# Two of seven half-size products of a down projection, each split once more into seven quarter-size products

## The chip, the cores and the metric

The kernel runs on one core of a Trainium2 chip. The engines of a core that matter here are TensorE (PE: matrix products; its weight loads are listed apart as PEld), VectorE (DVE), ScalarE (ACT) and GpSimd (POOL), each with a queue of instructions that it works off in order. SyncE (SP) only issues DMA transfers; POOL issues some too. The metric is the time of one execution on the device, in microseconds (us).

## The reference

One step of an encoder layer for 1024 prompt frames and 32 sample frames, 1056 tokens of width 1024. The layer ends in the squared-ReLU MLP with 4096 hidden features:

```python
def trunk_layer(x, ...):
    h = rms_norm(x, g_mix)
    z = h @ w_in                      # attention, convolution and gates
    ...
    x = x + (jax.nn.sigmoid(ga) * a + jax.nn.sigmoid(gb) * bo) @ w_mix_out
    ...
    x = x + co @ w_co                 # cross-attention
    hm = rms_norm(x, g_mlp)
    x = x + jnp.square(jax.nn.relu(hm @ w_up)) @ w_down
```

A last RMS norm gives the output. Everything is float32. The change is in the last line's product with `w_down`, 4096 by 1024.

## The kernel before

**Precision.** A float32 matrix product is made of three passes of a faster format: every operand is split into a high part (ACT casts it) and a low part (DVE subtracts the cast from the original), and TensorE sums high times high, high times low and low times high. `split`, lines 128 to 130, does so for the weights, `split_here`, lines 1316 to 1320, for an operand of the down projection in place.

**Layout.** Features lie on the 128 partitions, tokens along the row. In the down projection the tokens are two halves of `HT` = 528 columns, each of two quarters of `QT` = 264. A weight tile is 128 x 1024 floats (512 KB), eight blocks of 128 x 128.

**Seven half-size products.** Inner dimension (4096), outputs (1024) and tokens are halved. The eight products of halves are replaced by seven of sums of halves (Winograd's form of Strassen's scheme). The activations of each product are one of seven operands, named in `KINDS`: `b11`, `b21`, `b22` are halves themselves, `n1`, `n3`, `n4`, `t2` are sums. The up projection writes them to device memory (`op_d`), 16 tiles of 128 x 528 for each. The weights are a raw quarter of `w_down` (for `b11`, `b21`, `n4`) or a sum from `wsum_d` (for the others). `stage` (from line 1874) queues one product: 4 output tiles `j` times 2 halves `t` of the inner dimension, one weight tile for each of these eight steps, 48 matmuls with one weight tile (`part`, lines 1801 to 1811: 2 token quarters, 8 inner tiles, 3 passes). After the second half of a `j`, `to_x1` (from line 1788) adds the PSUM banks into the residual `x1` or subtracts them there, once for each place that the product belongs to; DVE does it, in up to three pieces for each since the residual is tiled in 384 tokens. Where a piece completes the residual, its square is added up for the last norm (ACT squares, POOL adds, lines 274 and 276).

**What runs beside it.** During a product, `pump2` fetches the operands of the next one by SyncE, three tiles a step, and splits them: per product 16 casts on ACT and 16 subtractions on DVE. `dslots` gives them their SBUF slots, alternating between two sets.

**Weights.** `next_w` keeps up to three split weights ready (`wh` and `wl` have three buffers each). `fetch_w` loads a raw tile into `wr`, which has two buffers here, on SyncE's queue (line 159).

**Sums of weights.** POOL makes them early, beside attention and gates: `pieces` (lines 708 to 710) lists 14 pieces for the gates, 32 for the down projection and 4 for the up projection. Each call of `sum_step` (lines 718 to 741) issues the load of one new piece and then, for the piece loaded by the call before, four additions and the store. Two tiles alternate: `ws`, and `xacc`, which later holds the sums of squares. All these instructions are pinned to their order among themselves. The 32 `hosts` (lines 743 to 777), one for each unit of attention, call it once each from the fourth on, on the second of three token chunks; later the output projection of attention and the gates call it again. `after_gates` ends this phase; then conv output and mix (`do_conv_out`, `do_mix`) use POOL for an addition for each tile (line 1069).

The order of instructions on each engine is made by a scheduler ahead of the run, from the order of the program text and estimated times; on the chip it is fixed.

## Time and profile before

| | us |
|---|---|
| three runs | 1746.15, 1753.02, 1753.42 |
| their median | 1753.02 |
| span of the profiled execution, first to last instruction | 1747.8 |
| ScalarE busy in it | 852.9 |
| GpSimd busy in it | 586.2 |
| VectorE busy in it | 1188.1 |

The down projection is the end of the span: its first matmul (line 1809) starts at 1400.6 us and its last at 1735.9 us; what follows is the last norm and the output. Its 2688 matmuls are 7 times 384. In a row of the profile, "idle before" is the time that the engine stood still just ahead of these instructions, with what ended most of it; a tile's name is written without its number, so `n` stands for `n1`, `n3` and `n4`. In a row of a timeline, the first number is the start in us from the begin of the span and the second the duration.

### The profile page before, as it was taken

The numbers are of one execution on the slowest core, as the hardware profiler recorded it, in microseconds if no ns is written. First come the engines' busy times: TensorE is split into PE (matmuls) and PEld (weight loads), VectorE is DVE, ScalarE is ACT, GpSimd is POOL, SyncE is SP. The second block draws the span as 40 slices with busy tenths as digits, with TensorE's granted clock in tenths as the row PEclk, the third lists the DMA queues.
The fourth block names the chain that finished last, engine by engine and source line by source line (L and its number), as shares of the span: only waits on it lengthen the run. The fifth ranks groups of instructions, "written<-read, shape, count | busy, mean of one in ns | idle before, by whom it ended". The sixth has DMA issues, their size and how long they took to land. (4 is left out here: it accounts for less than half of the span.)

```text
span 1747.8 us, 32606 instructions
## 1 busy us (share of the span) xinstructions
PE 1727.7 (99%) x12262; PEld 1712.4 (98%) x12262; DVE 1188.1 (68%) x2276; ACT 852.9 (49%) x1660; POOL 586.2 (34%) x667
## 2 busy tenths in 40 slices
PE   9999999999999999999999999999999999999998
PEld 8999999999999999999999999999999999999998
DVE  7776777768666646555677888787666686545675
ACT  8653534535335324434556666765444463332444
POOL 0026366443553544432224232005555410000121
PEclk9999999999999999999999999999999999999999
DMA  4333344333436888867766667775666695555554
GB/s 185 104 126 128 114 134 153 115 139 127 160 132 204 296 292 280 291 203 238 264 213 198 221 227 241 235 258 191 217 222 219 219 330 185 188 193 169 192 170 160
DMA packets 179854, 346.60 MB, mean 198 GB/s; under 512 B 18657, under 2 KB 101249, under 8 KB 179569
## 3 DMA queue, kind: packets, MB, share of 16 engines
q1 hardware_dynamic: 163504, 290.07, 50.0%
q0 software_dynamic: 15568, 53.68, 8.8%
q8 instruction: 96, 1.57, 0.4%
q10 hardware_dynamic: 624, 0.77, 0.1%
q14 instruction: 62, 0.50, 0.1%
HBM read 250.73 MB, written 93.14 MB: 197 GB/s over the span
## 5 line engine op out<-in xcount | busy, mean ns | idle before, releaser
L129 ACT CAST wh<-wr 128x1024 fp32r<-128x1024 f32 (+1 forms) x214 | 223.8, 1046 | 366.6 <-PE acc L1810 121.4
L130 DVE TENSOR_TENSOR wl<-wr,wh 128x1024 fp32r<-128x1024 f32 (+1 forms) x214 | 275.0, 1285 | 106.2 <-ACT wh L129 105.4
L200 PE MATMUL acc<-X,wh 128*128 128x384 f32 (+1 forms) x864 | 281.5, 326 | 0.0
L201 PE MATMUL acc<-X,wh 128*128 128x384 f32 (+1 forms) x864 | 278.8, 323 | 0.1
L202 PE MATMUL acc<-X,wl 128*128 128x384 f32 (+1 forms) x864 | 277.8, 322 | 0.0
L276 POOL TENSOR_TENSOR xacc<-xacc,ct 128x384 f32<-128x384 f32 (+1 forms) x56 | 75.6, 1354 | 379.9 <-ACT ct L274 378.1
L201 PEld LDWEIGHTS acc<-X,wh 128*128 128x128 f32 x864 | 162.7, 188 | 1.7 <-DVE X L280 0.7
L200 PEld LDWEIGHTS acc<-X,wh 128*128 128x128 f32 x864 | 162.4, 188 | 0.8
L202 PEld LDWEIGHTS acc<-X,wl 128*128 128x128 f32 x864 | 162.4, 188 | 0.1
L200 PE MATMUL acc<-Y,wh 128*128 128x384 f32 (+1 forms) x432 | 139.9, 326 | 3.2 <-DVE ct L1068 2.9
L202 PE MATMUL acc<-Y,wl 128*128 128x384 f32 (+1 forms) x432 | 140.0, 325 | 2.7 <-DMA wl<-wl_d 2.7
L201 PE MATMUL acc<-Y,wh 128*128 128x384 f32 (+1 forms) x432 | 139.7, 324 | 0.0
L129 ACT CAST PTh<-pt 128x512 fp32r<-128x512 f32 (+3 forms) x94 | 45.8, 516 | 112.8 <-PE pt L598 111.4
L1809 PE MATMUL acc<-n,wh 128*128 128x264 f32 x352 | 100.2, 285 | 0.0
L1810 PE MATMUL acc<-n,wh 128*128 128x264 f32 x352 | 100.1, 284 | 0.0
L1811 PE MATMUL acc<-n,wl 128*128 128x264 f32 x352 | 99.9, 284 | 0.0
L735 POOL TENSOR_TENSOR ws<-ws 128x256 f32<-128x256 f32 x100 | 89.5, 895 | 5.6
L735 POOL TENSOR_TENSOR xacc<-xacc 128x256 f32<-128x256 f32 x100 | 86.8, 868 | 5.7 <-DMA xacc<-in_w_in 0.4
L200 PEld LDWEIGHTS acc<-Y,wh 128*128 128x128 f32 x432 | 81.4, 189 | 4.4 <-DVE ct L1068 3.8
L202 PEld LDWEIGHTS acc<-Y,wl 128*128 128x128 f32 x432 | 81.5, 189 | 3.0 <-DMA wl<-wl_d 3.0
L201 PEld LDWEIGHTS acc<-Y,wh 128*128 128x128 f32 x432 | 81.6, 189 | 0.0
L584 ACT ACTIVATE S<-S,nmx 128x257 f32<-128x257 f32 (+1 forms) x132 | 64.2, 488 | 18.9 <-DVE nmx L579 17.6
(432 smaller groups left out, 5554.9 us busy)
## 6 DMA issues: line engine op xcount, KB each, us to landing
wr<-in_w_up SPq DMA_DIRECT2D x53, 512.0 KB, 4.5
wr<-in_w_in SPq DMA_DIRECT2D x52, 512.0 KB, 3.6
wr<-wsum_d SPq DMA_DIRECT2D x40, 512.0 KB, 3.5
wr<-in_w_conv_out SPq DMA_DIRECT2D x24, 512.0 KB, 3.9
wr<-in_w_mix SPq DMA_DIRECT2D x24, 512.0 KB, 5.2
wr<-in_w_down SPq DMA_DIRECT2D x24, 512.0 KB, 3.6
n_d<-Z SPq DMA_DIRECT2D x32, 264.0 KB, 4.2
xacc<-in_w_down POOLq DMA_DIRECT2D x16, 512.0 KB, 4.5
```

The source lines that it names most:

```text
L129: act.copy(hi, src)
L130: dve.tensor_sub(lo, src, hi.bitcast(F32))
L200: pe.matmul(out, wh[:, a], hi, start=(k == 0), stop=False)
L201: pe.matmul(out, wh[:, a], lo, start=False, stop=False)
L202: pe.matmul(out, wl[:, a], hi, start=False, stop=(k == len(acts) - 1))
L276: pool_e.tensor_tensor(acc, acc, sq, op=ALU.add)
L584: act.activation(stl[:, h, : nk + 1], stl[:, h, : nk + 1], AF.Exp, scale=-1.0, bias=nmx[:, h : h + 1], accum_out=den[:, h : h + 1],)
L735: pin(pool_e.tensor_tensor(t[:, to], t[:, x], t[:, y], op=ALU.add))
L1809: pe.matmul(a, wh[:, s], hi, start=(t == 0 and k == 0), stop=False, skip_group_check=True)
L1810: pe.matmul(a, wh[:, s], lo, start=False, stop=False, skip_group_check=True)
L1811: pe.matmul(a, wl[:, s], hi, start=False, stop=(t == 1 and k == 7), skip_group_check=True)
```

## The change

Products `b21` and `n4` are computed by the same scheme once more: inner dimension, outputs and tokens of the product are halved again, and seven quarter-size products P1 to P7 (8 inner tiles, 2 output tiles `i`, 264 tokens) take the place of eight. These two are products with a raw quarter of `w_down` that go to one place of the residual only. `t2` now comes ahead of `n4`: a product of the old kind stands before each.

- **More sums of weights.** 16 pieces (`w2`), made by the same `sum_step` with subtractions, stored in `w2_d`. Every second host from the sixth on gets a second call, on the third chunk: 14 calls.
- **Sums of operands.** During the product before (`b11`, `t2`), all 16 operand tiles are fetched in the first four steps (`prepare`); POOL makes three differences of quarters for each pair (`first_sums`) and writes them back by its own DMAs in place of the raw quarters; the first eight tiles are split (`near_split`), the two other sums go to tiles of their own (`extra_split`). That product runs its outputs in pairs, as `b11` did already: the first half of its operands is used for the last time two steps before its end.
- **The recursed stage** (`stage2`): 14 items, one weight tile each, 24 matmuls each. Sums of products that share a bank are made by accumulating into it; DVE or ACT takes a partial sum out in between (`after`). Beside them (`beside`) come the last sums of operands on POOL, their split, the raw quarters' split, and from the seventh item on the fetches for the next product.
- **Low halves on POOL.** `far_split` casts on ACT and subtracts on POOL: four tiles in each recursed stage, and eight of the 16 of the product behind it (`t2`, `n3`).
- Slots are given by tables (`HOMES`, `EXTRA`) in place of `dslots`.

```diff
+    RAW2 = {"b21": 1, "n4": 3}
+    w2_d = {kind: dram.tile([2, 4, P, 4, 256], F32, name=f"w2_{kind}") for kind in RAW2}
...
+    pieces += [("w2", kind, i, b) for kind in RAW2 for i in range(2) for b in range(4)]
...
+            elif at[0] == "w2":
+                _, kind, i, b = at
+                for r in range(2):
+                    pin(pool_e.dma_start(t[:, 2 * r : 2 * r + 2], io["w_down"][i + 2 * r, :, b, :, RAW2[kind]].rearrange("t p c -> p t c")))
...
-            for to, x, y in ((3, 2, 3), (2, 0, 2), (0, 0, 3), (1, 1, 0)):
-                pin(pool_e.tensor_tensor(t[:, to], t[:, x], t[:, y], op=ALU.add))
+            for to, x, y in ((3, 2, 3), (2, 0, 2), (0, 3, 0), (1, 1, 0)):
+                op = ALU.subtract if at[0] == "w2" and to != 3 else ALU.add
+                pin(pool_e.tensor_tensor(t[:, to], t[:, x], t[:, y], op=op))
...
+        if i % 2 and i > 4:
+            extras.append((2, sum_step))
...
-    KINDS = ["b11", "b21", "n4", "t2", "n3", "n1", "b22"]
+    KINDS = ["b11", "b21", "t2", "n4", "n3", "n1", "b22"]
...
+    def far_split(hi, lo):
+        raw = lo.bitcast(F32)
+        pin(act.copy(hi, raw))
+        pin(pool_e.tensor_tensor(lo, raw, hi.bitcast(F32), op=ALU.subtract))
...
+    def first_sums(kind, k):
+        (h0, x0), (h1, x1_) = ((hi.bitcast(F32), lo.bitcast(F32)) for hi, lo in (dn[kind, k], dn[kind, 8 + k]))
+        t = W["pool"].tile([P, 4, 256], F32, tag="ws", name=nm("ws")).rearrange("p q c -> p (q c)")[:, : 3 * QT]
+        t3, t2, t4 = (t[:, i * QT : i * QT + QT] for i in range(3))
+        pin(pool_e.tensor_tensor(t3, quarter(x1_, 1), quarter(x0, 1), op=ALU.subtract))
+        pin(pool_e.dma_start(quarter(x0, 1), t3))
+        pin(pool_e.tensor_tensor(t2, t3, quarter(x0, 0), op=ALU.add))
+        pin(pool_e.tensor_tensor(t4, quarter(x1_, 0), t2, op=ALU.subtract))
+        pin(pool_e.dma_start(h1, t[:, QT:]))
+    def extra_split(kind, k):
+        hi, lo = dn[kind, "e", k] = dpair(homes(EXTRA[kind])[k])
+        src = dn[kind, 8 + k][0].bitcast(F32)
+        pin(act.copy(hi, src))
+        pin(dve.tensor_sub(lo, src, hi.bitcast(F32)))
+    def last_sums(kind, m):
+        hi, lo = dn[kind, "f", m] = dpair(homes(EXTRA[kind])[8 + m])
+        for q in range(2):
+            h1, x1_ = (x.bitcast(F32) for x in dn[kind, 8 + 2 * m + q])
+            t = tmp(QT)
+            pool_e.tensor_tensor(t, quarter(x1_, 1), quarter(h1, 0), op=ALU.subtract)
+            pool_e.dma_start(quarter(lo.bitcast(F32), q), t)
+        return lambda: split_here(hi, lo)
...
+    def prepare(kind):
+        pairs = [(k, 8 + k) for k in range(8)]
+        at = {n: [] for n in range(8)}
+        for n in range(4):
+            at[n].append(lambda n=n: [fetch_op(kind, x) for pair in pairs[2 * n : 2 * n + 2] for x in pair])
+            at[n].append(lambda n=n: [first_sums(kind, k) for k in (2 * n, 2 * n + 1)])
+            at[n + 3].append(lambda n=n: [near_split(kind, k) for k in (2 * n, 2 * n + 1)])
+        for n in range(2):
+            at[6 + n].append(lambda n=n: [extra_split(kind, k) for k in range(4 * n, 4 * n + 4)])
+        return at
...
+    def stage2(kind, h, f0, last):
...
+        into = {"P1": "A", "P2": "A", "P6": "B", "P7": "B", "P4": "B", "P5": "C", "P3": "C"}
...
+        def beside(n):
+            if n < 2:
+                splits.extend(last_sums(kind, m) for m in (2 * n, 2 * n + 1))
+            elif 7 <= n < 9:
+                splits.pop(0)()
+                splits.pop(0)()
+            if 2 <= n < 6:
+                for k in (2 * n - 4, 2 * n - 3):
+                    (split_here if n < 4 else far_split)(*dn[kind, 8 + k])
+            if n == 4:
+                wanted2.extend((nxt, k) for k in range(16))
+            if 6 <= n:
+                pump2(2)
+        n = 0
+        for p in ("P1", "P6", "P7", "P4", "P2", "P5", "P3"):
+            for i in range(2):
+                def fn(w, p=p, i=i, n=n):
...
+                    for k in range(8):
+                        hi, lo = operand2(kind, p, k)
+                        s = slice(k * P, k * P + P)
+                        pe.matmul(a, wh[:, s], hi, start=(p in ("P1", "P6", "P5") and k == 0), stop=False, skip_group_check=True)
+                        pe.matmul(a, wh[:, s], lo, start=False, stop=False, skip_group_check=True)
+                        pe.matmul(a, wl[:, s], hi, start=False, stop=(k == 7), skip_group_check=True)
+                    after(p, i)
+                    beside(n)
...
-    stage("b21", ("w_down", 1), ((*A11, True, True),))
-    stage("n4", ("w_down", 3), ((*A21, True, False),))
+    stage2("b21", *A11, True)
     stage("t2", ("w_sum", 0), ((*A12, False, False), (*A21, True, False), (*A22, True, False)))
+    stage2("n4", *A21, False)
```

102 lines of the change are left out of this document (81 added, 21 removed).

## The prediction

> **What bounds the kernel now.** I began with the page: span, busy shares.
>
> ```profile
> span 1747.8 us, 32606 instructions
> ...
> PE 1727.7 (99%) x12262; PEld 1712.4 (98%) x12262; DVE 1188.1 (68%) x2276; ACT 852.9 (49%) x1660; POOL 586.2 (34%) x667
> ```
>
> TensorE sets the time. A busy share says little of pace, since ends are modelled, so I cut the down projection into stretches of 46.6 us, about one half-size product each (the first still holds the tail of the up projection; columns: stretch, then busy time and count of PE, PEld, DVE, ACT, POOL, then clock, DMA share, GB/s).
>
> ```profile
> 1402.00:1448.60 46.60, 46.60 (x385) 46.60 (x384) 38.41 (x70) 27.10 (x43) 4.84 (x3) 1.00 0.94 330
> 1448.60:1495.20 46.60, 46.60 (x385) 46.60 (x384) 29.47 (x55) 19.06 (x28) 3.21 (x2) 1.00 0.51 166
> ```
>
> A product is 4 output tiles x 16 inner tiles x 2 token quarters x 3 passes = 384 matmuls, and 385 start in each stretch, up to an edge: 46.6 / 384 = 0.1214 us each, without a gap, at full clock. VectorE (DVE) has 8 and 17 us to spare, GpSimd (POOL) over 40. So removed matmuls shorten the time directly, as long as the other engines still feed TensorE.
>
> **What is removed.** Seven quarter-size products are 7 x 2 output tiles x 8 inner tiles x 3 passes = 336 matmuls for 384. Twice 48 are saved: 96 x 0.1214 = **11.7 us**. That is the whole possible gain, 0.67%.
>
> **What is added to the two stages.** A recursed stage lasts 336 x 0.1214 = 40.8 us of TensorE. The prices (busy us and mean ns; count and min/median/max in ns; start and us; last the first stretch again for L1793 alone, the adds into the residual on DVE):
>
> ```profile
> L130 DVE TENSOR_TENSOR wl<-wr,wh 128x1024 fp32r<-128x1024 f32 x63 | 77.8, 1235 | 49.6 <-ACT wh L129 49.3
> ...
> L1538 DVE TENSOR_TENSOR Z<-Z,pc 128x264 f32<-128x264 f32 x2 | 0.8, 426 | 0.0
> ...
> L1320 DVE TENSOR_TENSOR n<-n,n x44: 694/700/1830, 1404.3 to 1682.6; 128x528 fp32r<-128x528 f32 x44
> ...
> L735 POOL TENSOR_TENSOR ws<-ws x100: 725/746/1742, 155.4 to 766.4; 128x256 f32<-128x256 f32 x100
> L730 POOL DMA_DIRECT2D ws<-in_w_down x16: 533/533/685, 347.9 to 712.3; - x16
> ...
> 1210.92 1.33 POOL L1574 TENSOR_TENSOR lt<-lt,Z 128x528 f32<-128x528 f32 x1
> ...
> 1402.00:1448.60 46.60, 7.18 (x28) 1.00 0.94 330
> ```
>
> DVE, per recursed stage: 14 weight splits at 1.23 us (there were 8, since a weight tile now serves 24 matmuls, not 48) = 17.2; 16 operand splits of 528 columns at 0.70 (4 of the last sums, 4 raw, 8 for the next product) = 11.2; 10 adds of a bank and a kept partial sum at 0.43 = 4.3; 12 pieces into the residual at 7.18 / 28 = 0.26 = 3.1. Together 35.8 of 40.8 us, 88%. ScalarE (ACT) casts alongside and, at 27 of 46.6 us in its fullest stretch, has more room. POOL, nearly idle before: 8 subtractions of a quarter at 0.75 (the 256-column row stands in for 264) = 6.0, 12 low halves that `far_split` takes from DVE at 1.33 = 16.0, and 8 DMA issues at 0.53 to 0.69.
>
> Neither sum passes 40.8. Their sharing is the question. These rows of the timeline show pairs that overlapped (start, duration):
>
> ```profile
> 1221.39 2.20 POOL L1568 TENSOR_TENSOR Z<-lt,Z 128x528 f32<-128x528 f32 x1 [2.45 <-DVE Z L1564]
> ...
> 1222.32 1.84 DVE L1566 TENSOR_TENSOR Z<-lt,Z 128x528 f32<-128x528 f32 x1
> ...
> 1478.29 1.64 POOL L276 TENSOR_TENSOR xacc<-xacc,ct 128x384 f32<-128x384 f32 x1 [62.26 <-ACT ct L274]
> ...
> 1478.97 1.52 DVE L1320 TENSOR_TENSOR n<-n,n 128x528 fp32r<-128x528 f32 x1
> ...
> 1216.27 1.29 POOL L1469 TENSOR_TENSOR s<-wr,s 128x512 f32<-128x512 f32 x1
> ...
> 1216.31 0.71 DVE L1519 TENSOR_TENSOR Z<-acc,lt 128x528 f32<-128x528 f32 x1 [2.62 <-PE pc L882]
> ```
>
> A DVE operation with both sources in SBUF takes 0.70 alone, but 1.84 and 1.52 beside a POOL one: it ends 0.57 and 0.56 us after POOL does, so it ran when POOL was through. With a PSUM source (last pair) it stays at 0.71. I therefore **add** POOL's arithmetic to DVE's two-SBUF work: 17.2 + 11.2 + 2.6 (the 10 residual pieces that come from a temporary) = 31.0, and POOL's 22.0, make 53.0 us in 40.8. Eight of the far halves (10.6 us) belong to the next product's second half and can run over into its first 11.7 us: 42.4. In `b21`'s stage 4 accumulations of squares (L276; 1.64 less the 0.68 before DVE's start, 0.96 each) add 3.8: 46.2. Excess: 5.4 us for `b21`, 1.6 for `n4`.
>
> The lead that could swallow it:
>
> ```profile
> wr<-in_w_down SPq DMA_DIRECT2D x24, 512.0 KB, 3.6
> ...
> 1459.17 1.05 ACT L129 CAST wh<-wr 128x1024 fp32r<-128x1024 f32 x1 [4.79 <-PE acc L1810]
> ```
>
> Today the cast waits for TensorE to give back a split tile, so splits run two tiles ahead: 2 x 24 x 0.1214 = 5.8 us less the split itself (2.3) is a lead of 3.5. A raw tile's round, issue to landing and split, is 3.6 + 1.05 + 1.23 = 5.9 us, over two raw tiles 2.94 us per weight against 2.91 wanted: this takes 14 x 0.03 = 0.4 of the lead and leaves no room for a late split. What waits in the end is a TensorE matmul on its `wl`, and all of TensorE's queue behind it. So `b21` stalls for 5.4 - 3.1 = 2.3 us and `n4` stays under its lead: **+2.3 us**. Bounds: 0 (DVE's order puts weights first) and 2 x (53.0 - 40.8) + 3.8 = 28.2 (nothing slides, no lead).
>
> **Preparation beside the product before.** POOL gets 24 subtractions (18.0 us) and 16 issues (8.8 at 0.55) into `b11`'s 46.6 us, and again into `t2`'s. DVE's count stays there: 16 splits for 16. In the first stretch DVE's 38.4 less 7.2 (residual adds, from PSUM), POOL's 4.8 of before and the new 18.0 make 54.0 in 46.6: 7.4 too much. Data are also late there: 330 GB/s x 46.6 us is 15.4 MB, and the writes back from SBUF to SBUF add 8 x 405 KB = 3.3 MB; at the highest rate near it,
>
> ```profile
> 1410.00:1420.00 10.00, 10.00 (x84) 10.00 (x83) 9.89 (x12) 6.62 (x11) 3.52 (x2) 1.00 1.05 388
> ```
>
> that is 18.7 / 388 = 48 us. The first quarter product needs all eight near splits within 3 us of its start. Of 0 to 7.4 I take **+3.0**, since much of DVE's work there is the tail of the up projection; in `t2`'s stretch, if like the second row (166 GB/s, 29.5 us of DVE), nothing. No wait is added on TensorE apart from these operands and the banks: the second sum into a bank waits for DVE's reading of the first, with 24 matmuls (2.9 us) between.
>
> At this place a rule of the Trainium skill speaks against the change. "SBUF — State Buffer", section "SBUF: two separate sides", says that a DMA issued by GpSimd can starve, because its descriptors can't be written while VectorE holds the shared port, and gives 3.1 us instead of 0.62. By it, 16 issues would take 50 us, an estimate from that page, and the preparation would miss its product. The L730 row has a largest issue of 0.685 us among 16, and the row of 117 to 523 us below has DVE 71% busy, so this trace doesn't show it; I keep it as rival 4.
>
> **The earlier stages.** Sixteen pieces of summed weights join the 50 that POOL makes beside attention and gates, each two loads, four additions and a store. SyncE's queue is not touched there. The chain:
>
> ```profile
> 277.33 1.45 POOL L728 DMA_DIRECT2D xacc<-in_w_in  x2 [2.93 <-DMA gsum_d<-xacc]
> 287.00 1.45 POOL L728 DMA_DIRECT2D ws<-in_w_in  x2 [2.57 <-DMA gsum_d<-ws]
> ...
> 802.09 1.00 POOL L1069 TENSOR_TENSOR ct<-ct,ct 128x384 f32<-128x384 f32 x1 [32.96 <-DMA wr<-in_w_conv_out]
> ...
> 117.00:523.00 406.00, 406.00 (x2627) 399.96 (x2627) 287.40 (x721) 172.43 (x426) 203.57 (x303) 1.00 0.40 133
> ...
> 844.87 0.51 ACT L274 ACTIVATE xacc<-Ga 128x384 f32<-128x384 f32 x1
> ```
>
> Back to back a step takes 9.7 us, and each load waits for a store's landing, with POOL's queue (the attention's small copies, the convolution's products) behind it. From 117 to 523 us 29 of the steps ran (by the timeline's loads), 281 us. POOL's other work there is 203.6 less 29 x 5.2 (four additions at 0.75, and issues of 1.1 to 2.9) = 53. That leaves 406 - 281 - 53 = 72 us, 7 steps; the other 9 come after the old end, 769 us (802.1 less the idle 33.0), at 769 + 87 = 856 us. TensorE itself has no slack, but nothing waits for these sums until 1448. What does wait is the tile: `xacc` is written at 844.9, and L1069 stands in POOL's queue from 802, then late behind blocked loads. Bounds: 0 (they fit between) and 8 convolution outputs each 4 us later, 32; by the row at 844.9, 11 us before that end, where a single cast waits and TensorE has convolution outputs beside it, I take **+1.0**.
>
> **Sum:** -11.7 + 2.3 + 3.0 + 1.0 = **-5.4 us** on a span of 1747.8. The three runs shown are 1746.15, 1753.02 and 1753.42: the span lies between, and what is around it isn't shown, so I carry the difference to the median: 1753.0 - 5.4 = **1747.6 us**. Half a per cent, about what a measurement of this kernel can tell from no change, is 8.8 us.
>
> **Rivals.**
> 1. *The lead holds and the preparation is in time: the whole gain stays.* For it: both engines are under 100% taken singly, and from 117 to 523 us POOL is busy half of the time and DVE 71% beside a full TensorE. Against: POOL's work there is not needed at once. Time: 1753.0 - 11.7 + 1 = 1742.3. Chance 0.31.
> 2. *VectorE and GpSimd in turn become the bound in both recursed stages* (slower). It decides where the far halves don't slide: 28.2 + 4.0 - 11.7 = +20.5, 1773.5; it passes no change once the stall is over 7.7 us, and 0.5% from 16.5. Chance 0.11.
> 3. *The chain of sums ends past the gates and holds the residual stage* (slower). It decides from the end of the chain at about 845 us: 8 x 4 = 32 for the 1.0 gives 1747.6 + 31 = 1779; half of it 1763. Chance 0.08.
> 4. *POOL's DMA issues starve behind DVE.* Each of 16 issues waits one weight split (1.23): 19.7 us late before `b21`, little before `n4`, whose stretch has 20 us free: 1747.6 + 19.7 - 3.0 = 1764. Chance 0.04.
>
> Forecast: partial stall, 0.46, its own range 1745 to 1758. Faster by over 0.5% is rival 1 (0.31), within is the forecast (0.46), slower is 2 to 4 (0.23). The range takes in rival 1, with half of the 7 us by which the runs above spread, rival 4 and the smaller half of 2 and 3: 1738 to 1768.
>
> **What would show it.** Right: 336 matmuls in each recursed stage, its length 41 to 47 us, DVE near 90%, POOL at half, TensorE waiting on `wl` there. Wrong: a length of 40.8 (rival 1); over 50, or overlapped splits of 2 us throughout (2); the chain's last store after 845 us and fewer matmuls per 10 us from 800 to 880 (3); POOL issues of over 1 us before `b21` (4). A stall in the attention hosts, which I cost at nothing because TensorE shows none and DVE has 119 of 406 us free, would be an error of mine.

## The result and the profile after

The changed kernel takes 1843.5 us (median of 5 runs, 1840.7 to 1846.1) where the kernel before takes 1746.2 (5 runs): a ratio of 1.054, 95% interval 1.052 to 1.056. The forecast was 1747.6, at most 1768. Rows of the changed kernel bear its own line numbers: `first_sums` is L1660 to L1664 (L1661 and L1664 issue its two write-backs), splits on ACT and DVE are L1334/1335, extra splits L1672/1673, weight splits L131/132, the recursed matmuls L2038 to 2040, their additions L2000 and L2009, the chain of sums L738 to L752, and POOL's addition in the convolution's output, L1069 before, is L1084.

The profiled execution has a span of 1839.0 us against 1747.8, 91.2 more. Two marks divide it: the first and the last matmul into `pc`, the up projection. They stand at 1174.50 and 1407.57 us before, and at 1191.82 and 1424.86 after. So **17.3 us** are lost ahead of the up projection, none in it, and **73.9 us** behind it, where 96 matmuls fewer should have given 11.7 back: 85.6 us of stall.

The first loss, in the timeline of the changed kernel (start, length, engine, line, operation; in brackets the idle time before and what ended it):

```profile
814.71 3.13 POOL L746 TENSOR_TENSOR ws<-ws 128x256 f32<-128x256 f32 x4
818.15 0.59 POOL L752 DMA_DIRECT2D w_n<-ws  x1 [0.31 <-POOL ws L746]
818.76 1.00 POOL L1084 TENSOR_TENSOR ct<-ct,ct 128x384 f32<-128x384 f32 x1
819.80 0.51 ACT L131 CAST M<-ct 128x384 fp32r<-128x384 f32 x1 [18.65 <-POOL ct L1084]
821.72 0.69 PE L205 MATMUL acc<-Y,wh 128*128 128x384 f32 x1 [10.52 <-ACT wh L131]
```

The chain of sums makes its last store at 818.15 us (before: 767.69), and only then does GpSimd reach the addition behind it, which ran at 802.09 before. ScalarE's queue stands for 18.65 us on that addition, with weight casts behind it, and TensorE for 10.52 on one of those casts.

The second loss, in the waits of TensorE from 1425 to 1660 us (waiter, what it waited for, us in total, times, longest):

```profile
PE acc L2038 <- ACT Z L1334: 24.6, 4, 8.0
PE acc L2038 <- ACT n L1334: 21.1, 4, 7.7
PE acc L2038 <- DVE ct L2000: 5.5, 8, 0.9
PE acc L2038 <- DVE ct L2009: 4.5, 2, 2.6
```

The recursed stages' first quarter products wait 45.7 us for the near splits. What those wait for shows in the timeline of GpSimd and ScalarE within the first of these stretches:

```profile
1483.78 0.55 POOL L1664 DMA_DIRECT2D H<-ws  x1 [0.41 <-POOL ws L1663]
1484.24 0.63 ACT L1334 CAST Z<-Z 128x528 fp32r<-128x528 f32 x1 [4.73 <-DMA Z<-ws]
1490.04 0.74 POOL L1660 TENSOR_TENSOR ws<-H,Z 128x264 f32<-128x264 f32 x1 [5.70 <-DMA H<-ws]
1493.85 0.63 ACT L1334 CAST Z<-Z 128x528 fp32r<-128x528 f32 x1 [3.30 <-DMA Z<-ws]
1494.87 0.56 POOL L1664 DMA_DIRECT2D H<-ws  x1 [0.41 <-POOL ws L1663]
1497.36 0.73 POOL L1660 TENSOR_TENSOR ws<-H,Z 128x264 f32<-128x264 f32 x1 [1.93 <-DMA H<-ws]
1504.90 0.73 POOL L1660 TENSOR_TENSOR ws<-H,Z 128x264 f32<-128x264 f32 x1 [2.14 <-issue]
```

The first sums of a pair start only when the write-back of the pair before has landed, since `ws` is one tile: 7.3 and 7.5 us from one start to the next in the last three rows of L1660, 13.5 ahead of them (the start before is at 1476.53), where the arithmetic is 2.3 us. That is not the whole of it: the first pair stands 8.0 us ahead of issuing its write-back, for a reason that the profile doesn't name. The eight pairs run from 1431.47 to 1509.73 us, 78 us, beside a product of 46.6; ahead of `n4` they run from 1573.57 to 1636.09, 62.5 us. Beside their ends TensorE stands, as the last four of these stretches of the changed kernel show; the first row lies in the first loss (stretch and length, then busy us and count of PE, PEld, DVE, ACT and POOL, granted clock, DMA share, GB/s):

```profile
810.00:820.00 10.00, 1.20 (x7) 0.88 (x6) 0.00 (x0) 0.20 (x1) 8.51 (x12) 0.67 0.37 136
...
1480.00:1490.00 10.00, 1.40 (x3) 0.79 (x3) 3.48 (x9) 0.71 (x2) 3.89 (x6) 0.62 0.78 260
1490.00:1500.00 10.00, 1.40 (x3) 0.79 (x3) 2.20 (x3) 1.82 (x3) 7.56 (x11) 0.50 0.14 54
1500.00:1510.00 10.00, 1.96 (x5) 1.11 (x5) 2.27 (x3) 2.52 (x5) 6.98 (x11) 0.50 0.22 82
...
1620.00:1630.00 10.00, 2.09 (x5) 1.29 (x5) 1.46 (x2) 1.26 (x2) 5.29 (x8) 0.50 0.40 145
```

A full stretch of the down projection has 84 matmuls; in the last four rows there are 3 to 5. There no engine is busy throughout, and the DMA share is as low as 0.14: a chain of short steps, each waiting for the one before, not a lack of throughput.

### The profile page after: what moved, and what is told of

It is laid out like the page before. It is cut to its first block, busy times and chain, and to the rows that moved or that the text cites. A ratio compares the mean times of both kernels' runs of the same rounds, so it can differ in the third digit from the quotient of the medians.

```text
span 1839.0 us, 32903 instructions
## 1 busy us (share of the span) xinstructions
PE 1739.7 (95%) x12166; PEld 1711.4 (93%) x12166; DVE 1251.1 (68%) x2308; ACT 881.9 (48%) x1700; POOL 788.0 (43%) x915
## 5 line engine op out<-in xcount | busy, mean ns | idle before, releaser
L131 ACT CAST wh<-wr 128x1024 fp32r<-128x1024 f32 (+1 forms) x226 | 236.1, 1045 | 324.8 <-PE acc L206 77.3
L132 DVE TENSOR_TENSOR wl<-wr,wh 128x1024 fp32r<-128x1024 f32 (+1 forms) x226 | 297.4, 1317 | 109.4 <-ACT wh L131 108.2
L746 POOL TENSOR_TENSOR ws<-ws 128x256 f32<-128x256 f32 x132 | 114.9, 870 | 7.0
L746 POOL TENSOR_TENSOR xacc<-xacc 128x256 f32<-128x256 f32 x132 | 111.4, 844 | 7.5 <-DMA xacc<-in_w_in 0.2
L131 ACT CAST PTh<-pt 128x512 fp32r<-128x512 f32 (+3 forms) x94 | 45.8, 517 | 104.7 <-PE pt L603 103.4
L1871 PE MATMUL acc<-n,wh 128*128 128x264 f32 x256 | 73.4, 287 | 0.0
L1870 PE MATMUL acc<-n,wh 128*128 128x264 f32 x256 | 73.3, 286 | 0.0
L1872 PE MATMUL acc<-n,wl 128*128 128x264 f32 x256 | 73.3, 286 | 0.0
```

The lines of the kernel that those rows point to most:

```text
L131: act.copy(hi, src)
L132: dve.tensor_sub(lo, src, hi.bitcast(F32))
L746: pin(pool_e.tensor_tensor(t[:, to], t[:, x], t[:, y], op=op))
L1870: pe.matmul(a, wh[:, s], hi, start=(t == 0 and k == 0), stop=False, skip_group_check=True)
L1871: pe.matmul(a, wh[:, s], lo, start=False, stop=False, skip_group_check=True)
L1872: pe.matmul(a, wl[:, s], hi, start=False, stop=(t == 1 and k == 7), skip_group_check=True)
```

## The experiments

One table first. "Up from" is the first matmul into `pc`, "up" the time to the last one, "rest" from there to the end of the span, all of the profiled execution, in us; the medians and ratios to the kernel before are of all runs. Among kernels whose early stages are alike, "up from" ranges by some 10 us (1190 to 1200), so a difference of a few us in that column says nothing. "Rest" differs by some 3 us where the down projection is alike (414.1 and 417.4, 361.3 and 364.5).

| kernel | up from | up | rest | median | ratio (95%) |
|---|---|---|---|---|---|
| before | 1174.5 | 233.1 | 340.2 | 1746.2 | |
| the change | 1191.8 | 233.0 | 414.1 | 1843.5 | 1.054 (1.052–1.056) |
| e1 sums only | 1207.6 | 233.1 | 340.2 | 1771.3 | 1.015 (1.012–1.019) |
| e2 two temporaries | 1196.4 | 233.0 | 387.2 | 1817.5 | 1.041 (1.039–1.043) |
| e3 in place | 1190.0 | 233.0 | 361.6 | 1789.3 | 1.025 (1.023–1.026) |
| e4 sums in the up projection | 1169.7 | 265.7 | 424.0 | 1864.1 | 1.067 (1.065–1.069) |
| e5 more calls | 1181.3 | 233.0 | 417.4 | 1833.3 | 1.049 (1.047–1.051) |
| e6 SyncE issues | 1190.5 | 233.1 | 406.5 | 1831.2 | 1.048 (1.046–1.050) |
| e7 in place, spread | 1196.9 | 233.0 | 361.3 | 1795.3 | 1.027 (1.025–1.029) |
| e8 e7 + calls | 1179.5 | 233.1 | 364.5 | 1782.4 | 1.020 (1.019–1.022) |
| e9 in place, no subtractions | 1190.9 | 233.0 | 358.8 | 1785.0 | 1.023 (1.020–1.026) |
| e10 in place, no first sums | 1193.7 | 233.0 | 362.1 | 1790.2 | 1.025 (1.023–1.028) |
| e11 both left out | 1192.5 | 233.0 | 358.7 | 1788.6 | 1.025 (1.022–1.029) |
| e12 in place, third raw tile | 1200.3 | 233.0 | 362.8 | 1791.1 | 1.025 (1.021–1.029) |
| e13 e8 + third raw tile | 1185.8 | 233.1 | 361.1 | 1777.7 | 1.017 (1.014–1.019) |
| e14 in place, one-bank tiles | 1197.8 | 233.0 | 366.8 | 1791.7 | 1.026 (1.023–1.029) |
| e15 e14 + third tile + calls | 1177.5 | 233.1 | 355.1 | 1775.5 | 1.017 (1.015–1.020) |
| e16 e2 + one-bank tiles + calls | 1182.0 | 233.1 | 386.4 | 1803.6 | 1.032 (1.029–1.034) |
| e17 e15, no subtractions | 1185.5 | 233.0 | 349.8 | 1769.0 | 1.012 (1.011–1.014) |

### The chain of sums: e1, e4, e5

e1 adds to the kernel before only the pieces and their calls, and uses none of them:

```
+    pieces += [("w2", kind, i, b) for kind in RAW2 for i in range(2) for b in range(4)]
...
+        if i % 2 and i > 4:
+            extras.append((2, sum_step))
```

> The kernel before, to which only the sixteen extra pieces of weight sums of the change are added, made and written to DRAM at the same places, and read by nothing; the down projection is that of before. Theory: the chain of sums on GpSimd, longer by sixteen pieces, ends past the first gates and holds back GpSimd's additions of the convolution, so this alone costs what the changed kernel is behind at the start of its up projection: 1746 + 15 to 18, that is 1761 to 1764, with the last store of the chain near 818 us. Rival: what is late there is caught up later, or the changed attention hosts have nothing to do with it: 1746 to 1750.

It took 1771.3 us, 24.6 over the 1746.6 of the kernel before beside it, with the same 340.2 us behind the up projection. The theory's mechanism holds and its price was too low; the rival falls. In the timeline of e1 (its L743, L749 and L1081 are the chain's addition and store and the convolution's addition):

```profile
826.27 3.13 POOL L743 TENSOR_TENSOR ws<-ws 128x256 f32<-128x256 f32 x4
829.72 0.59 POOL L749 DMA_DIRECT2D w_n<-ws  x1 [0.31 <-POOL ws L743]
830.33 1.00 POOL L1081 TENSOR_TENSOR ct<-ct,ct 128x384 f32<-128x384 f32 x1
```

The chain ends still later here than in the changed kernel, 829.7 instead of 818.2 us; why these two differ wasn't tried. The profiled execution is also the longest of e1's four, 1782.7 us where the others took 1767.4 to 1771.8, so its 33.1 us ahead of the up projection are more than the sums usually cost.

e4 takes the pieces out of the early stages and makes one at each pair of the up projection:

```
-    pieces += [("w2", kind, i, b) for kind in RAW2 for i in range(2) for b in range(4)]
+    pieces2 = [("w2", kind, i, b) for kind in RAW2 for i in range(2) for b in range(4)]
...
+        if i == 0:
+            pieces.extend(pieces2)
+        sum_step()
         c = [ps.tile([P, 512], F32, tag="pt", bufs=2, name=nm("pc"))[:, :QT] for _ in range(2)]
```

> The changed kernel, whose sixteen pieces of weight sums are made in the up projection, one at each of its pairs, in place of beside the attention and the first gates; the calls of the chain before are those of the kernel before. Theory: the late chain costs the changed kernel 15 to 18 us, and in the up projection the sums cost nothing: 1825 to 1828. Rival: GpSimd is needed as much in the up projection, and the loss only moves there: 1840 to 1846.

It took 1864.1 us, slower than both said. The early stages have their time back (the up projection starts at 1169.7, 22 us sooner than in the changed kernel), but the up projection grows by 32.6 us and what follows by 9.9. The stretch of the up projection in e4, then its longest entry in the waits of TensorE there, an entry in those of ScalarE, and VectorE's weight splits in e4 (1170 to 1436 us) and in the changed kernel (1192 to 1424 us; count, busy us, mean ns, idle before):

```profile
1175.00:1430.00 255.00, 231.80 (x1819) 227.34 (x1818) 173.70 (x190) 107.44 (x143) 206.89 (x183) 0.97 0.73 246
```

```profile
PE acc L895 <- DVE wl L1498: 17.1, 11, 4.1
```

```profile
ACT wh L1495 <- POOL s L1483: 13.4, 8, 2.3
```

```profile
L1498 DVE TENSOR_TENSOR wl<-s,wh 128x1024 fp32r<-128x1024 f32 x30 | 53.2, 1773 | 15.7 <-ACT wh L1495 15.7
```

```profile
L1500 DVE TENSOR_TENSOR wl<-s,wh 128x1024 fp32r<-128x1024 f32 x30 | 36.5, 1216 | 0.6 <-ACT wh L1497 0.6
```

GpSimd is busy for 207 of 255 us, and TensorE waits for VectorE's weight splits (L1498). They are late in two ways: each lasts 1.77 us instead of 1.22, and ScalarE's casts ahead of them wait 13.4 us for `s`, the sums of the up projection's own weights that GpSimd makes there, which they never do in the changed kernel. How much each of the two costs wasn't tried. In the changed kernel GpSimd has 125 of 225 us there. That nearly half of a helper's time is free does not make the place free.

e5 leaves the pieces where they are and gives the chain three more calls among the attention heads:

```
-        if i % 2 and i > 4:
+        if i % 2 and i > 4 or i in (12, 20, 28):
```

> The changed kernel with three more calls of the chain of sums beside the attention (17 extra ones for the 16 pieces, where the change has 14). Theory: the chain ends late (818 us, before 768) not because GpSimd has no time for it, but because with 14 extra calls its last steps are the last calls there are, right ahead of the gates' end; with three calls more among the attention it ends near 770 again, GpSimd's additions of the convolution start as before, and the 17 us behind at the start of the up projection go: 1824 to 1829. Rival: GpSimd beside the attention is full, the calls only queue up and the chain ends as late as now: 1838 to 1850.

1833.3 us, between the two: 10 us come back, all of them ahead of the up projection, but the last store is still at 810.47 us. The table bears the 10 us out: the six kernels with these calls start their up projection at 1177.5 to 1185.8 us, the ten that have the sums there without them (e1 aside) at 1190.0 to 1200.3. So part of the lateness is that the chain ran out of calls, and part is the chain's own pace, where each load waits for a store to land (6.71 us of GpSimd idle before the load at 809.11 us in the changed kernel's timeline).

### The write-back of the first sums: e2, e3, e6

e2 gives the first sums two tiles in turn:

```
-        t = W["pool"].tile([P, 4, 256], F32, tag="ws", name=nm("ws")).rearrange("p q c -> p (q c)")[:, : 3 * QT]
+        t3 = tmp(QT)
+        t2_4 = W["pool"].tile(...)[:, :HT] if k % 2 else S["f"].tile([P, HT], F32, tag="fs", name=nm("fs"))
```

> The changed kernel, whose first sums have two temporary tiles in turn for t2 and t4 (the old one and a new one) and the eviction ring's tiles for t3, in place of one tile for all. Theory: each pair of pieces waits for the write-back of the pair before to land, since there is one tile, and that makes the eight pairs 78 and 62 us long beside a product of 41 to 47; with two tiles a pair can start 4 to 5 us sooner, so the two preparations shrink by some 20 to 30 us each and the time falls to 1785 to 1810. Rival: GpSimd's own three subtractions and two issues for a pair (4.5 to 6 us) in turn with VectorE's work set the pace; then the second tile brings under 10 us: 1833 to 1843.

e3 does without tile and write-back; the sums go straight to their place, rounded:

```
-        pin(pool_e.tensor_tensor(t3, quarter(x1_, 1), quarter(x0, 1), op=ALU.subtract))
-        pin(pool_e.dma_start(quarter(x0, 1), t3))
...
+        pin(pool_e.tensor_tensor(quarter(dn[kind, k][1], 1), quarter(x1_, 1), quarter(x0, 1), op=ALU.subtract))
+        pin(pool_e.tensor_tensor(quarter(dn[kind, 8 + k][0], 0), quarter(x0, 1), quarter(x0, 0), op=ALU.add))
+        pin(pool_e.tensor_tensor(quarter(dn[kind, 8 + k][0], 1), quarter(x1_, 0), quarter(h1, 0), op=ALU.subtract))
```

> The changed kernel, whose GpSimd writes the first sums straight to where the write-back put them, as operands rounded for TensorE: no temporary tile, no write-back, two DMAs a pair fewer; the sums lose their low parts, which the output's error shows. Theory: with the wait for the write-back gone altogether the preparation goes at GpSimd's pace, 2.3 to 3.7 us a pair and inside the products of b11 and t2, so that nearly all of the stall before P1 goes (65 to 75 us of the 85 that the down projection is longer): 1768 to 1780. Rival: GpSimd and VectorE excluding one another set the pace, and the waits for the DMAs only covered this: 1820 or more.

e2 took 1817.5 us, 26 less than the change but 8 more than the theory's range; e3 took 1789.3, 54 less, 9 over its range. Both rivals are far off. GpSimd in the timeline of e2, at the same pairs (L1661 starts a pair, L1665 writes it back):

```profile
1469.02 0.74 POOL L1661 TENSOR_TENSOR ct<-H,Z 128x264 f32<-128x264 f32 x1 [3.21 <-DMA H<-b_d]
...
1474.20 0.76 POOL L1661 TENSOR_TENSOR ct<-H,Z 128x264 f32<-128x264 f32 x1
...
1478.53 0.77 POOL L1661 TENSOR_TENSOR ct<-H,Z 128x264 f32<-128x264 f32 x1
```

A pair now starts 4.3 to 5.2 us after the one before, at GpSimd's own pace of three operations and two issues, and no longer waits for the landing of the one before. Behind the up projection the change, e2 and e3 take 414.1, 387.2 and 361.6 us: waiting for the one tile is 26.9 us of it, and what is left of the write-back with two tiles (issue, landing ahead of the near splits, the place in GpSimd's queue) another 25.6, which these runs don't divide further. The place in the queue shows in the last pair of e2: it starts at 1483.23 us and issues its write-back only at 1494.46, with seven subtractions and five issues of the last sums between, 8.2 us; ahead of `n4` it is 1597.62 and 1609.55.

e6 keeps the tile and lets SyncE issue the two write-backs:

```
-        pin(pool_e.dma_start(quarter(x0, 1), t3))
+        sp.dma_start(quarter(x0, 1), t3)
...
-        pin(pool_e.dma_start(h1, t[:, QT:]))
+        sp.dma_start(h1, t[:, QT:])
```

> The changed kernel, whose two write-backs of the first sums are issued by SyncE in place of GpSimd; the one temporary tile stays. Theory: the next pair still waits for the landing of the write-back before, so the eight pairs take about as long (now 78 and 62 us): 1830 to 1850. Rival: the issues on GpSimd's queue (0.55 us each, behind VectorE's accesses) are what is slow; without them the down projection gets back 30 us or more: 1790 to 1815.

1831.2 us: at the theory's near end, and far from the rival's 1790 to 1815. The 12 us may come from the 1.1 us of issues a pair that are off GpSimd's queue, or from the changed order; these weren't separated.

### The other 33 us: e7 to e17

With in-place sums the down projection still takes 361.6 us where 340.2 less 11.7 were expected, 33.1 more. Stretches of e3 in its first recursed stage:

```profile
1480.00:1490.00 10.00, 7.48 (x49) 6.96 (x48) 8.78 (x18) 4.65 (x7) 0.00 (x0) 0.83 0.38 123
1490.00:1500.00 10.00, 8.07 (x63) 7.51 (x61) 7.54 (x9) 6.69 (x10) 5.66 (x4) 1.00 0.69 212
...
1510.00:1520.00 10.00, 6.25 (x46) 5.85 (x45) 9.50 (x16) 3.68 (x7) 0.00 (x0) 0.95 0.82 286
1520.00:1530.00 10.00, 9.38 (x68) 9.20 (x67) 7.18 (x13) 5.96 (x10) 3.93 (x3) 0.88 0.93 302
```

Against 84 in a full stretch these four lack 110 matmuls, 13.4 us at 0.1214. The second stage lacks 106 from 1580 to 1630 us, and `b11` 51 from 1440 to 1460: together 32.4 us. What `b11` loses stands behind these waits of ScalarE and TensorE in e3:

```profile
1445.27 1.04 ACT L131 CAST wh<-wr 128x1024 fp32r<-128x1024 f32 x1 [7.22 <-DMA wr<-in_w_down]
1450.26 0.39 PE L1868 MATMUL acc<-t,wl 128*128 128x264 f32 x1 [2.06 <-DVE wl L132]
```

A raw weight tile lands late there, after 20 us with a DMA share of 1.03 and 1.02, in which `prepare` fetches the operands; the cast waits 7.22 us for it, and TensorE for the split behind. No run below changes these fetches. For the two stages four suspects followed, one after the other.

**Bursts of splits.** e7 spreads them over the stage, e8 adds e5's calls:

```
-            elif 7 <= n < 9:
-                splits.pop(0)()
-                splits.pop(0)()
+            elif 4 <= n < 8:
+                splits.pop(0)()
...
-            if 6 <= n:
-                pump2(2)
+            if 2 <= n:
+                pump2(2 if n > 5 and n % 2 == 0 else 1)
```

> The kernel of in-place first sums (no temporary tile, no write-back, the sums rounded), whose other preparation within a recursed stage is spread out: the last sums are split one for each half product from the fifth on (there, two at the eighth and two at the ninth), and the next stage's sixteen operands are fetched and split from the third half product on, one or two each (there, two each from the seventh on). Theory: of the 33 us that the down projection still loses with in-place sums, some 14 are banks that wait for VectorE's additions behind bursts of four splits (46 and 45 matmuls in 10 us of 84 there); spread out, 8 to 14 us come back: 1775 to 1781. Rival: VectorE's work in a recursed stage as such, twice as many weight splits for a matmul, is what is too much; wherever the splits stand, the same time is lost: 1785 to 1793.

> In-place first sums, the preparation within the recursed stages spread out, and three more calls of the chain of sums, all in one. Theory: the gains add up, since they lie in different stages: 1789 less 17 for the chain less 8 to 14 for the spreading, 1758 to 1764; still above the kernel before by what the start of the b11 stage and the weights' loads lose. Rival: what comes back ahead of the down projection is lost again in it, as when the sums were made in the up projection: 1775 or more.

The rest takes 361.3 us in e7, as in e3, and the median is 6 us more: spreading gives nothing, and the theory falls. In e8 the calls bring 13 us of the 17 expected of them; the 1782 us belong to its rival's range, because the spreading's share never came.

**VectorE's and GpSimd's work.** e9 leaves out VectorE's subtractions of 12 splits a stage, e10 GpSimd's first sums, e11 both (near split and first sums shown):

```
-        split_here(*dn[kind, k])
+        hi, lo = dn[kind, k]
+        pin(act.copy(hi, lo.bitcast(F32)))
...
-        pin(pool_e.tensor_tensor(quarter(dn[kind, k][1], 1), quarter(x1_, 1), quarter(x0, 1), op=ALU.subtract))
...
+        pin(act.copy(dn[kind, 8 + k][0], x1_))
```

> In-place first sums, with VectorE's subtractions of the near splits (8 a stage) and of the last sums' splits (4 a stage) left out: the low parts of these operands stay the unsplit values. Theory: what the in-place kernel still loses within the two recursed stages, 13 us each, is banks and operands that wait for VectorE, whose work there is near 9 tenths of the time; 12 subtractions of 0.66 to 1.2 us each are 8 to 14 us of it, and with them gone 10 to 24 us come back: 1765 to 1779. Rival: the weights' loads, late behind the operands', hold these stages, and VectorE only waits for them too: 1784 to 1791.

> In-place first sums, with GpSimd's three operations a pair left out (the 24 of each preparation); ScalarE copies x into the place of two of the sums in their stead, so the sums aren't made. Theory: with the write-back gone, these operations cost nothing in the products of b11 and t2 they lie beside (7 us lost in b11, 0 in t2, and the 7 by weights that load behind the operands): 1783 to 1792. Rival: GpSimd's operations lengthen VectorE's beside them (0.66 to 1.2 us for a split), and so make VectorE late for the recursed stage: 1765 to 1779.

> In-place first sums, with both left out: VectorE's subtractions of the near and last splits, and GpSimd's operations of the first sums. Theory: as the run without the subtractions alone, within 5 us. Rival: GpSimd and VectorE share the loss, so leaving out both gives 10 us or more beyond the better of the two single runs.

1785.0, 1790.2 and 1788.6 us: e9's theory falls, e10's holds, and e11 is no better than e9, as its theory says. As long as the rest is as in e3, neither VectorE's splits nor GpSimd's first sums set the time. GpSimd's other work beside VectorE, the low halves of `far_split`, was left out in no run.

**Two raw weight tiles.** e12 gives the down projection a third:

```
+        third.update(n=0, pool=W["pool"])
...
-                    kept2["s"] = W["pool"].tile([P, 4, 256], F32, tag="ws", ...)
+                    kept2["s"] = S["f"].tile([P, HT], F32, tag="fs", name=nm("fs"))
```

> In-place first sums, and a third tile for raw weights in the whole down projection (the tile that the in-place sums no longer need; the recursed stages' kept sums of P1 move to a small tile of their own). Theory: the remaining 33 us are the supply of weights: a half product of a recursed stage lasts 2.9 us, and a raw tile is taken for its load (2 to 5 us among the operands' loads), ScalarE's copy (1.05) and VectorE's subtraction (1.23) with the waits between them, over 5.8 us for a round, so two tiles don't supply one weight each 2.9 us; with three, 12 to 25 us come back: 1764 to 1777. Rival: ScalarE and VectorE take the weights up late because they stand in order behind splits and additions, whatever the number of tiles: 1782 to 1792.

> In-place first sums, a third tile for raw weights, three more calls of the chain of sums, and the preparation within the recursed stages spread out. Theory: the causes found account for all of the difference: 1789 less 10 to 17 for the chain less 12 to 25 for the weights, 1747 to 1767, that is level with the kernel before or up to 1.2% above it. Rival: the weights aren't it, and this is as the run with the calls and the spreading alone: 1776 to 1784.

1791.1 us, and e13 1777.7: this theory falls as well. Yet the trace shows that the tile did what it should. ScalarE's longest waits from 1470 to 1545 us, in e3:

```profile
ACT wh L131 <- DMA wr<-w_b: 13.4, 6, 5.2
```

and in e12:

```profile
ACT wh L131 <- PE acc L2037: 16.3, 8, 3.9
```

Weights came late before; now they wait for TensorE to give back a split tile, and TensorE is as late as ever. In the timeline of e12, TensorE's first matmul of a half product and the reading by VectorE (L1998) that ends its wait:

```profile
1498.74 0.43 DVE L1998 TENSOR_TENSOR ct<-acc,fs 128x264 f32<-128x264 f32 x1 [0.44 <-PE acc L2038]
1499.22 0.39 PE L2036 MATMUL acc<-t,wh 128*128 128x264 f32 x1 [0.53 <-DVE ct L1998]
1502.46 0.43 DVE L1998 TENSOR_TENSOR ct<-acc,fs 128x264 f32<-128x264 f32 x1 [0.92 <-PE acc L2038]
1503.04 0.36 PE L2036 MATMUL acc<-n,wh 128*128 128x264 f32 x1 [0.61 <-DVE ct L1998]
1506.33 0.42 DVE L1998 TENSOR_TENSOR ct<-acc,fs 128x264 f32<-128x264 f32 x1
1506.90 0.36 PE L2036 MATMUL acc<-n,wh 128*128 128x264 f32 x1 [0.70 <-DVE ct L1998]
```

VectorE waits for the end of a half product, reads it, and only then does the next one start, each 3.8 us where 24 matmuls take 2.9. Four half products in a row do so in each of the two stages, 5.9 us of waits in all. The next half product writes the other bank, and has nothing to do with that reading; but both banks are one tile, `banks[into[p]]`, and the wait seems to go by the tile, which e14 tries.

**Banks in pairs.** e14 takes tiles of one bank; e15 adds the third raw tile and the calls; e16 does it with e2's full-precision sums and the calls:

```
-                        banks[into[p]] = wide_tile()
+                        banks[into[p]] = wide_tile() if p == "P1" else [ps.tile([P, 512], F32, tag="pt", bufs=2, name=nm("pt")) for _ in range(2)]
```

> In-place first sums, and the sums of P6, P7, P4 and of P5, P3 in two tiles of one bank each in place of one tile of two banks. Theory: a half product waits until VectorE has read the half product just ahead of it, though that one went to the other bank, since both banks are one tile; eight or nine such waits in a recursed stage, each 0.6 to 0.7 us and 0.2 us of restart, are 7 to 8 us a stage. With tiles of one bank 10 to 18 us come back: 1771 to 1779. Rival: VectorE is late itself, and the wait only moves to the next reading of the same bank: 1784 to 1792.

> In-place first sums, tiles of one bank, a third tile for raw weights, and three more calls of the chain of sums. Theory: the causes add up: 1789 less 10 to 17 for the chain, 10 to 18 for the banks and 0 to 8 for the weights, which had no room to show while the banks held each half product: 1748 to 1768. Rival: what one gives the next takes, 1770 or more.

> The changed kernel with full-precision first sums through two temporary tiles, tiles of one bank, and three more calls of the chain of sums. Theory: 1817.5 less 10 to 17 for the chain and 10 to 18 for the banks: 1783 to 1798. Rival: the wait for the write-backs takes the banks' gain, since the first half products wait for the near splits anyway: 1800 to 1808.

e14 took 1791.7 us, in its rival's range, and the rest of its profiled execution, the longest of its four, is even 5 us longer than e3's. The regular waits of 0.6 us, four a stage and not the eight or nine that its expectation counted, are gone but for one of 0.5, so they did go by the tile; but others stand in their place. Two stretches of e14, then the longest wait of TensorE in the second:

```profile
1500.00:1510.00 10.00, 9.96 (x83) 9.75 (x81) 6.55 (x10) 5.28 (x7) 6.86 (x4) 1.00 0.86 282
1510.00:1520.00 10.00, 4.97 (x31) 4.57 (x32) 5.89 (x9) 3.36 (x6) 0.00 (x0) 0.87 1.03 350
```

```profile
1518.47 0.56 PE L2034 MATMUL acc<-lt,wh 128*128 128x264 f32 x1 [4.29 <-DVE Ga L1850]
```

The first is nearly full now. In the second the DMA share is 1.03, with the next product's operands under way, and TensorE does 31 matmuls. Only together with the third raw tile, in e15, does the rest come down to 355.1 us; the median of 1775.5 is the rival's, its runs 1767.8 to 1781.3. e16's 1803.6 is the rival's too.

In e15's first recursed stage VectorE is busy for 8 to 10 of each 10 us. e17 leaves out e9's subtractions once more, now without the other limits:

> In-place first sums, tiles of one bank, a third tile for raw weights, three more calls of the chain of sums, and VectorE's subtractions of the near splits (8 a stage) and of the last sums' splits (4 a stage) left out. Theory: VectorE is the next limit once the others are gone, and was masked in the run that left only its subtractions out: 8 to 14 us less work a stage gives 10 to 20 us of the 27 that are left: 1755 to 1765. Rival: what is left is the loads of weights behind the operands' loads, and VectorE waits for them: 1770 to 1778.

1769.0 us, above the theory's range and just below the rival's. The rest takes 349.8 us, 5.3 less than in e15, where the same step from e3 to e9 gave 2.8. Against a scatter of some 3 us this suggests that VectorE's splits are one of the limits; it does not prove it. The recursed stages themselves, from first to last matmul, take 46.0 and 43.7 us now, where they take 57.8 and 57.1 in e3 (some 24 matmuls of the next product, 2.9 us, lie among those of e3). Stretches of e17 with the most missing:

```profile
1440.00:1450.00 10.00, 6.91 (x34) 6.19 (x33) 7.69 (x15) 5.27 (x7) 9.84 (x11) 0.67 0.51 161
...
1510.00:1520.00 10.00, 7.92 (x62) 7.50 (x62) 9.69 (x13) 7.48 (x12) 6.71 (x5) 1.00 1.07 366
...
1610.00:1620.00 10.00, 6.66 (x42) 6.67 (x43) 9.93 (x12) 2.56 (x4) 7.12 (x5) 0.83 0.40 135
```

Against 84 each they lack 114 matmuls, 13.8 us. They lie in `b11`, at the end of the first recursed stage and behind the second. In `b11` the raw weights land late as in e3 (a cast at 1441.03 us follows a landing at 1440.93); in the middle one the DMA share is above 1 and ScalarE waits for weights too. Behind the second stage it is VectorE that is late (GpSimd's `far_split`, VectorE's splits of an operand and of a weight, and the matmul that waits for the last):

```profile
1604.26 6.22 POOL L1642 TENSOR_TENSOR n<-n,n 128x528 fp32r<-128x528 f32 x4 [16.47 <-ACT n L1641]
1607.49 3.55 DVE L1335 TENSOR_TENSOR n<-n,n 128x528 fp32r<-128x528 f32 x2
1610.97 2.31 DVE L132 TENSOR_TENSOR wl<-wr,wh 128x1024 fp32r<-128x1024 f32 x1
1613.34 0.39 PE L1871 MATMUL acc<-t,wl 128*128 128x264 f32 x1 [4.18 <-DVE wl L132]
```

Two operand splits that take 0.70 us each alone last 3.55 us beside GpSimd, the weight's split 2.31 instead of 1.23, and TensorE stands for 4.18. All this is read from the trace: neither the order of the loads nor `far_split` was tried. Of 33.1 us, 11.8 are accounted for by e17's changes together; how the other 21.3 divide stays open. No version was level with the kernel before.

## Why the prediction was wrong

**-11.7, right in count.** Each recursed stage has 336 matmuls, and at the full clock a matmul still takes 0.1214 us. But such a stage lasts 85.7 us in the changed kernel (first P1 matmul at 1478.37, last of P3 at 1564.06; some 24 matmuls of the next product lie among them) and 80 the second time, far above the 41 to 47 that would have shown the forecast right.

**+3.0 for the preparation beside the product before is the step that failed.** The text weighed 54.0 us of DVE and POOL work against 46.6 us, and 18.7 MB against a rate, and from 0 to 7.4 us it took 3.0, with nothing ahead of `n4`. Both are sums of work. The eight pairs are a chain through one tile: arithmetic, issue, landing, next pair. That is 78 us and 62.5 us for eight pairs, whatever share of any engine is free. The code shows the one buffer, and the prediction quoted rows in which the chain of weight sums waits for a store's landing in just that way (2.57 and 2.93 us idle), but used them only for that other chain. By e3 it cost **52.5 us** (414.1 less 361.6) behind the up projection; e10 and e11 show that the arithmetic that was weighed costs nothing there. What `b11` still loses with in-place sums, 6.2 us, is weights that land late: the prediction counted the bytes, but not whom they delay.

**"No wait is added on TensorE apart from these operands and the banks"**, and for a bank "24 matmuls (2.9 us) between": wrong at the second half. Both banks of a pair are one tile, so there were no matmuls between; four half products in a row in each stage waited for the reading of the one just ahead (e12's timeline).

**+2.3 for the stall in the recursed stages: mis-sized.** With in-place sums each of them lacks some 13 us. The count of 88% for VectorE and the raw tiles' "2.94 us per weight against 2.91 wanted" were right as warnings and wrong as a result: the text added the excess of one limit and let a lead absorb it, where waits for banks, weights, operand loads and VectorE's order stand close behind one another, and what one gives up the next takes (e7, e9, e12 and e14 alone give nothing or near it; e15 and e17 give 6.5 and 11.8 us). Rival 2's price for both stages, 28.2, was close to the size, but its cause was VectorE and GpSimd excluding one another, and leaving out GpSimd's first sums (e10) or VectorE's splits (e9) brought little or nothing back; with the other limits gone (e17) VectorE's splits brought 5.3 us, not far beyond the scatter. That cause is not excluded: behind the second stage of e17 `far_split` holds VectorE in just this way for some 4 us, and no run was without it.

**+1.0 for the chain of sums: the mechanism was rival 3's, at an earlier date than the text allowed.** Its end was forecast at 856 us and came at 818; its cost was forecast to start with the tile `xacc` at 845, and it started at 802, where L1069 stood in GpSimd's queue behind the chain. The prediction wrote that L1069 was "late behind blocked loads" and then priced another wait. Measured: 17.3 us in the changed kernel, 15.5 to 25.8 in the later kernels with the same early stages, 24.6 alone (e1, by the medians). That nothing waits for the sums themselves until 1448 was true, and beside the point: what waits is what stands behind them on an engine that works in order.

**Rival 4 was not shown.** It drew on the Trainium skill, "SBUF — State Buffer", section "SBUF: two separate sides", by which GpSimd's DMAs can starve while VectorE holds the port that they share. The issues of the write-backs, from 1425 to 1515 us of the changed kernel (line, operation, count, busy us, mean ns, idle before):

```profile
L1664 POOL DMA_DIRECT2D H<-ws x6 | 3.3, 556 | 2.4 <-POOL ws L1663 2.4
```

take 0.56 us each, near the 0.53 to 0.69 before the change. What was slow is the landing: these write-backs land 2.3 to 6.1 us after their issue, and 2.2 to 5.6 us after it in e6, where SyncE issues them and GpSimd still waits for them. So the starving is not the cause.

The attention hosts lost little, as forecast: 302 matmuls against 321 from 300 to 350 us, and elsewhere up to 800 us the counts of 50 us differ by at most 13, to either side. From 800 to 850 us there are 210 against 288.

## What to carry to other kernels

Before adding steps that use one temporary tile again and again, multiply the whole round (arithmetic, issue, landing, next start) by their number and compare that with the stage they lie beside; sums of busy time and bytes can't show it. Work that nothing waits for still delays all that stands behind it on its engine, so price it by the next instruction that someone does wait for. When matmul groups are made half as long, every wait for each group (a weight split, a bank's reading, a tile shared by two banks) comes twice as often with half the cover, and taking one of them away may, as here, only show the next.

## What was not expected of the hardware

A starved TensorE also loses clock. In the stretches of 3 to 5 matmuls above the granted clock falls to 0.62 and then 0.50, a matmul there lasts 0.59 us instead of 0.28, and the first one after a wait of only 0.6 us lasts 0.36 to 0.39. A long stall thus costs more than its length: behind the one that ends at 1509.43 us in the changed kernel, the next eight matmuls start within 2.46 us, where full clock takes 0.97. Over the whole run the mean granted clock is 0.975 for the changed kernel and 0.989 for e3.

GpSimd at 81% (e4, 207 of 255 us) goes with a late VectorE: 17.1 us of TensorE's waits are on VectorE's weight splits, though VectorE itself was busy for only 174 of the 255. A VectorE operation with both sources in SBUF is longer beside GpSimd's arithmetic, as the prediction read from two pairs of rows: 1.77 us on average instead of 1.22 for these splits, and 1.8 instead of 0.70 for an operand's split in e17.
